# A three-stage float32 network on one core: norm roots on GpSimd, ordered weight subtractions, padded rows, another start

## The chip, the cores and the metric

One NeuronCore of one Trainium2 chip. TensorE (PE) multiplies, with a weight-load stream of its own (PEld); VectorE (DVE), ScalarE (ACT) and GpSimd (POOL) do the elementwise work; SyncE (SP) issues nearly all DMAs. The metric is the device time of one execution in microseconds; lower is better.

## The reference, cut to what matters

256 tokens of width 1024 pass a first block (gated linear attention and block attention, then a feed-forward that picks 16 of 16384 experts per head) and a second block of two layers. Everything is float32. Between the stages stands, eight times, the same norm:

```
def rmsnorm(x, w):
    y = x * rsqrt(mean(x * x, axis=-1) + 1e-6)
    return y * w
h = h + mixer(rmsnorm(h, mix_norm))
h = h + conv_glu_ffn(rmsnorm(h, ffn_norm))
h = h + sigmoid(rmsnorm(h, ple_norm) @ ple_gate) * (p @ ple_proj)
```

The order of the stages is: first mixer, norm, experts (peer), norm, mixer ab, norm, feed-forward 0, norm, gate stage (ple) 0, norm, mixer c, norm, feed-forward 1, norm, gate stage 1.

## The kernel before, in words

*Tiles.* The tokens lie in two tiles of 128 rows (tile 0 and tile 1), h[0] and h[1]. A stage's input is the normalised h, transposed and kept in two parts: xTh, rounded to PE's fast float32 format, and xTl, the rest (xT for both). The mixers' outputs go to mT in the same form and the feed-forward's hidden rows to hT.

*Weights.* wload (L102 to L114) brings a block of 128x1024 by DMA into a ring tile raw (512 KB), ACT copies it to hi in the fast format (L109), and DVE, or in the peer stage at times GpSimd, subtracts to get lo (L112). A product is made of three PE instructions: hi with the high part, lo with the high part, hi with the low part. xs (L169) has the tokens as the stationary operand and 512 weight columns streaming past (L199 to L201); ws (L245) has the weights stationary and 256 tokens streaming (L258 to L260); peer_v (L909) is like xs.

*The hand-over between stages.* The last products of a stage (hold) are made for tile 0 first and then for tile 1. When tile 0's sums are done they are added to h (add_epi, L269) and norm_tile (L314) starts: ACT squares two halves with a running sum (L320), rsqrt (L271) makes the reciprocal root on DVE from ten instructions on 128x1 (L278 to L288, a first guess by integer arithmetic and a polynomial), and DVE makes xn = h * r * weight in three cuts of 256, 256 and 512 columns (L326). turn then transposes xn on PE into PSUM (L338), ACT copies the high part to xTh (L292) and DVE subtracts the low part to xTl (L293); turn is deferred by some steps (D_N) or flushed. Then tile 1 follows. The next stage's first weight group is made for tile 0 before tile 1, so PE can start on tile 0 alone; feed-forwards start with ple_proj, which does not read xT.

*Order.* The program is written in emission order, and a scheduler of the tile framework puts each engine's instructions into one queue by its own estimate of when they are ready; earlier emitted work has the higher priority. Each queue then runs in order. A later subtraction of the next stage's weights (L112) can therefore stand inside a norm's root if the scheduler thinks it is ready there.

*The start.* load_x (L368) issues on SP, in this order: h[0], the identity, the norm weights broadcast to 128 partitions (norm_w, L309), two weight blocks, h[1], two more weight blocks; after them come the constants of the first block and the second weight group.

*Places in memory.* Tiles are laid out pool by pool in the order in which pools are opened; pads (wpad, tpad) exist in the weight ring's pool and in the pool of small tiles. After the peer stage a pool cc is opened for good (build, L1387 on) with kw (128x64) and sink (128x2x16), float32, and the pools of mixer ab, feed-forward 0, gate 0, mixer c, feed-forward 1 and gate 1 are opened on top of it; xT and the weight ring lie below it.

Of the kernel before, what the change touches and what calls it, by code (L numbers as in the profile page):

```python
# [9 lines left out]
F32 = mybir.dt.float32  # L10
F32R = mybir.dt.float32r
# [31 lines left out]
def f32(ap):  # L43
    return ap.bitcast(F32)


class Net:
    def __init__(self, ctx, tc, T):
        self.ctx, self.tc, self.nc, self.T = ctx, tc, tc.nc, T
        e = ctx.enter_context  # L50
        self.const = e(tc.tile_pool(name="const", bufs=1))
        self.res = e(tc.tile_pool(name="res", bufs=1))
        self.wp = e(tc.tile_pool(name="wp", bufs=1))
        self.tiny = e(tc.tile_pool(name="tiny", bufs=3))
# [6 lines left out]
        self.turn, self.wx = {}, None  # L61
        self.deferred = []
        self.lo_pattern = "V"
        self.u_pattern = "G"
        self.v_pattern = "VG"
# [33 lines left out]
        self.wx = None  # L99


    def wload(self, src, width=2048):  # L102
        nc = self.nc
        out = []
        for a in range(0, width, 1024):
            raw = self.ring("raw", F32)
            nc.sync.dma_start(raw, src[:, a:a + 1024])
            hi, lo = self.ring("hi", F32R), self.ring("lo", F32R)
            nc.scalar.activation(hi, raw, AF.Copy)  # L109
            eng = nc.vector if self.lo_pattern[self.lo_i % len(self.lo_pattern)] == "V" else nc.gpsimd  # L110
            self.lo_i += 1
            eng.tensor_tensor(lo, raw, f32(hi), op=ALU.subtract)  # L112
            out.append((hi, lo))
        return out  # L114

    def defer(self, ticks, f, norm=False):

# [48 lines left out]
            except StopIteration:  # L166
                gens.remove(x)

    def xs(self, xT, seq, epi, hold=0, norm=None, ready=()):  # L169
# [39 lines left out]
        for tt in range(2):  # L209
            if not tt and norm is not None:  # L210
                wb = self.norm_w(norm)
            if tt:
                self.flush_norm()
            for i in range(max(early, 0), len(order)):
                step(i, tt)
                yield
            if norm is not None:
                self.norm_tile(tt, wb)

    def preload(self, seq):  # L220
        return [x for src, width, _ in seq for x in self.wload(src, width)]

    def group(self, src, c):
        return [(src[q], 2048, [(c, 2 * q), (c, 2 * q + 1)]) for q in range(2)]
# [4 lines left out]

    def out_proj(self, xT, src, first, epi, hold, norm):  # L230

        g = self.xs(xT, self.cross(src, first) + self.cross(src, 1 - first), epi, hold, norm)
# [57 lines left out]

    def split(self, dh, dl, p):
        self.nc.scalar.activation(dh, p, AF.Copy)  # L292
        self.nc.vector.tensor_tensor(dl, p, f32(dh), op=ALU.subtract)  # L293

    def bcast(self, pool, src, name, w=D):
        t = pool.tile([P, w], F32, name=name)
# [14 lines left out]
        self.nc.sync.dma_start(wb, bass.AP(tensor=w.tensor, offset=w.offset, ap=[[0, P], [1, D]]))  # L311
        return wb

    def norm_tile(self, tt, wb):  # L314

        nc, h, pool, xT = self.nc, self.h, self.np_pool, self.xT
        ss = self.tiny.tile([P, 2], F32, tag="ss", name=self.nm("ss"))
        for c in range(2):
            junk = pool.tile([P, 512], BF, tag="junk", name=self.nm("junk"))
            nc.scalar.activation(junk, h[tt][:, c * 512:c * 512 + 512], AF.Square, scale=1.0 / 32, accum_out=ss[:, c:c + 1])  # L320
        r = self.rsqrt(1, ss[:, :1], add=ss[:, 1:])
        xn = []
        for k, n in NORM_CUTS:
            cs = slice(k * P, (k + n) * P)
            x = pool.tile([P, n * P], F32, tag=f"xn{n}", bufs=2, name=self.nm("xn"))
            nc.vector.scalar_tensor_tensor(x, h[tt][:, cs], r, wb[:, cs], op0=ALU.mult, op1=ALU.mult)  # L326
            xn.append((x, k, n))

        def turn():
            for x, k, n in xn:  # L330
                self.tsplit(x, xT, k, tt, n)
        self.defer(D_N[tt], turn, True)


    def tsplit(self, src, xT, k0, tt, n=4, pin=False):
        p = self.sm_ps()[:, :n * P]
        for j in range(n):
            x = self.nc.tensor.transpose(p[:, j * P:(j + 1) * P], src[:, j * P:(j + 1) * P], self.ident)  # L338
# [4 lines left out]
        self.split(xT[0][:, k0:k0 + n, t], xT[1][:, k0:k0 + n, t], p3)  # L343

    def headnorm(self, dst, src, H, w, pool):

# [15 lines left out]
    def consts(self):  # L362
        nc, T, c = self.nc, self.T, self.const
        self.ident = c.tile([P, P], F32, name="ident")
        nc.sync.dma_start(self.ident, T["c_ident"])


    def load_x(self, between=lambda: None):  # L368
        nc, T = self.nc, self.T
        self.h = h = [self.res.tile([P, D], F32, tag=f"h{t}", name=self.nm("h")) for t in range(2)]  # L370
        nc.sync.dma_start(h[0], T["x"][:P, :])
        self.consts()
        r = between()
        nc.sync.dma_start(h[1], T["x"][P:, :])
        return r

    def block1(self):
        T = self.T
        seq = self.group(T["w_in_xs"][0], 0)
        wb, ready = self.load_x(lambda: (self.norm_w(T["norm1_w"]), self.preload(seq[:1])))  # L380
        ready += self.preload(seq[1:])
        h = self.h
        with ExitStack() as st:
            self.psum(st, **PS1)
            pool = st.enter_context(self.tc.tile_pool(name="b1x", bufs=1, reuse_waits="tile"))
            mT = self.new_xT(pool, "mT")
            for tt in range(2):
                self.norm_tile(tt, wb)
            self.flush()
            xT = self.xT  # L390
# [695 lines left out]
    def hg_scores(self, qs, kk, b, lbt, reset, lmask, dmask, at, ax, t2, t4, pool):  # L1086

        nc = self.nc
# [295 lines left out]
    def build(self):  # L1384
# [3 lines left out]
        for f, *args in ((self.peer,), (self.mixer_ab, 0), (self.ffn, 0), (self.ple, 0, False),  # L1388
# [114 lines left out]
```

## Time and profile before

| | us |
|---|---|
| runs, median of 3 (lowest to highest) | 1665.56 (1662.08 to 1666.26) |
| profiled execution, its own time | 1669.8 |
| its span in the profile | 1667.9 |
| PE busy | 1622.6 (97%) |
| DVE busy | 1223.6 (73%) |
| ACT busy | 942.6 (57%) |
| POOL busy | 271.9 (16%) |

The span is the time from the first to the last instruction in the profile; the execution's own time includes what lies around it. PE counts as busy while a product is in the array, and products overlap: the distance of two starts tells the pace. The granted clock of 1.00 is TensorE's higher level.

### The profile page before, as it was taken

To read this page: it belongs to the slowest core of one execution; us is meant where nothing else is said; L and a number is where in the kernel's file an instruction comes from. 1 tells how busy PE (TensorE), PEld (TensorE's weight loads), DVE (VectorE), ACT (ScalarE), POOL (GpSimd) and SP (SyncE) were. 2 spreads that over 40 slices of the span, in tenths; PEclk is the share of its full clock that TensorE was granted. 3 is DMA by queue.
4 is the path that set the end of the run, shared out by engine and by line. 5 is a ranking of instruction groups with operands and counts; after the bars stand their busy time and mean duration, and the time that the engine had idled before them with its cause. 6 is when DMAs were issued, how large, how long until landed. Compare 5 with 4: busy or idle time off the path is not lost.

```text
span 1667.9 us, 27611 instructions
## 1 busy us (share of the span) xinstructions
PE 1622.6 (97%) x10592; PEld 1450.4 (87%) x10592; DVE 1223.6 (73%) x2300; ACT 942.6 (57%) x1435; POOL 271.9 (16%) x127
## 2 busy tenths in 40 slices
PE   6999999999999999999999999999999899999998
PEld 5877999999999988888888889769998677899986
DVE  7766597908999996655666568878894775688846
ACT  4555545456766665555555556556663555566633
POOL 1000499983333310000000000100000000000000
PEclk9999999999999999999999999999999998999999
DMA  7536456554444456557665554346665651465651
GB/s 262 174 126 193 161 167 198 167 166 140 140 149 130 145 171 196 194 191 239 203 192 195 192 183 149 127 138 191 192 196 185 219 168 58 128 189 185 185 189 62
DMA packets 83199, 285.07 MB, mean 171 GB/s; under 512 B 10555, under 2 KB 14588, under 8 KB 82940
## 3 DMA queue, kind: packets, MB, share of 16 engines
q1 hardware_dynamic: 83068, 283.31, 52.9%
q8 instruction: 83, 1.36, 0.3%
q14 instruction: 48, 0.39, 0.1%
HBM read 281.16 MB, written 2.12 MB: 170 GB/s over the span
## 4 chain that ended last, share of the span: by engine, by line
PE 79%; DVE 16%; ACT 2%; issue 1%; DMA 1%; SPq 0%; DVEq 0%; ACTq 0%
PE mm L909 21%; PE mm L258 11%; PE mm L259 11%; PE mm L260 11%; PE mm L199 6%; PE mm L201 6%; PE mm L200 6%; DVE h L869 5%; DVE lo L112 4%; DVE E L863 2%; DVE act L879 1%; PE sm L557 1%; PE sm L873 1%; PE sm L338 1%; PE sm L529 1%
## 5 line engine op out<-in xcount | busy, mean ns | idle before, releaser
L109 ACT ACTIVATE hi<-raw 128x1024 fp32r<-128x1024 f32 x513 | 541.7, 1058 | 343.4 <-PE mm L259 151.1
L112 DVE TENSOR_TENSOR lo<-raw,hi 128x1024 fp32r<-128x1024 f32 x417 | 512.0, 1230 | 196.1 <-ACT hi L109 193.8
L258 PE MATMUL mm<-xTh,hi 128*128 128x256 f32 x1992 | 560.4, 281 | 0.2
L259 PE MATMUL mm<-xTl,hi 128*128 128x256 f32 x1992 | 554.0, 278 | 0.0
L260 PE MATMUL mm<-xTh,lo 128*128 128x256 f32 x1992 | 553.8, 278 | 0.0
L258 PEld LDWEIGHTS mm<-xTh,hi 128*128 128x128 f32 x1992 | 375.4, 189 | 1.5 <-ACT xTh L292 0.7
L260 PEld LDWEIGHTS mm<-xTh,lo 128*128 128x128 f32 x1992 | 375.5, 189 | 0.2
L259 PEld LDWEIGHTS mm<-xTl,hi 128*128 128x128 f32 x1992 | 374.4, 188 | 0.5 <-DVE xTl L293 0.3
L112 POOL TENSOR_TENSOR lo<-raw,hi 128x1024 fp32r<-128x1024 f32 x96 | 249.1, 2610 | 241.2 <-ACT hi L109 230.8
L869 DVE TENSOR_TENSOR h<-E,gate 128x512 f32<-128x512 bf16 x64 | 116.0, 1814 | 1.8 <-PE sm L873 1.8
L199 PE MATMUL mm<-hi,xTh 128*128 128x512 f32 x256 | 105.8, 414 | 2.8 <-DVE ry L281 1.9
L200 PE MATMUL mm<-lo,xTh 128*128 128x512 f32 x256 | 102.6, 401 | 0.3 <-DVE lo L112 0.3
L201 PE MATMUL mm<-hi,xTl 128*128 128x512 f32 x256 | 102.4, 401 | 0.0
L868 ACT ACTIVATE h<-E 128x512 f32<-128x512 bf16 x64 | 72.4, 1134 | 43.3 <-DVE E L863 41.6
L1331 DVE SCALAR_TENSOR_TENSOR fc<-mm,cw,fc 128x255 f32<-128x255 f32 (+1 forms) x176 | 84.3, 479 | 3.1
L909 PE MATMUL mm<-hi,xTh 128*128 128x512 f32 x256 | 79.5, 391 | 1.5 <-DVE act L839 1.0
L863 DVE TENSOR_TENSOR E<-sel,iota 128x1024 bf16<-128x1024 bf16 x64 | 48.5, 796 | 43.7 <-POOL iota L857 38.1
L909 PE MATMUL mm<-hi,xTl 128*128 128x512 f32 x256 | 80.0, 393 | 0.0
L909 PE MATMUL mm<-hi,wl 128*128 128x512 f32 x256 | 79.8, 393 | 0.0
L909 PE MATMUL mm<-lo,xTh 128*128 128x512 f32 x256 | 79.5, 391 | 0.0
L909 PE MATMUL mm<-lo,wh 128*128 128x512 f32 x256 | 79.3, 391 | 0.0
L909 PE MATMUL mm<-hi,wh 128*128 128x512 f32 x256 | 79.1, 390 | 0.0
(294 smaller groups left out, 2306.8 us busy)
## 6 DMA issues: line engine op xcount, KB each, us to landing
raw<-in_peer_uT SPq DMA_DIRECT2D x128, 512.0 KB, 3.8
raw<-in_peer_v SPq DMA_DIRECT2D x128, 512.0 KB, 3.6
raw<-in_ffn_up_ws SPq DMA_DIRECT2D x88, 512.0 KB, 4.4
raw<-in_ffn_down_a SPq DMA_DIRECT2D x40, 512.0 KB, 4.5
raw<-in_w_in_xs SPq DMA_DIRECT2D x20, 512.0 KB, 4.7
raw<-in_ab_ws SPq DMA_DIRECT2D x16, 512.0 KB, 4.5
raw<-in_ple_gate_xs SPq DMA_DIRECT2D x16, 512.0 KB, 4.4
raw<-in_w_query_ws SPq DMA_DIRECT2D x12, 512.0 KB, 4.5
```

The source lines that it names most:

```text
L109: nc.scalar.activation(hi, raw, AF.Copy)
L112: eng.tensor_tensor(lo, raw, f32(hi), op=ALU.subtract)
L199: nc.tensor.matmul(p, xh[:, k, t], hi[:, w], start=n == 1 and kk == 0, stop=False)
L200: nc.tensor.matmul(p, xh[:, k, t], lo[:, w], start=False, stop=False)
L201: nc.tensor.matmul(p, xl[:, k, t], hi[:, w], start=False, stop=n == total[c] and kk == 1)
L258: nc.tensor.matmul(o, hi[:, w], xh[:, k, :], start=k == 0, stop=False)
L259: nc.tensor.matmul(o, hi[:, w], xl[:, k, :], start=False, stop=False)
L260: nc.tensor.matmul(o, lo[:, w], xh[:, k, :], start=False, stop=k == 7)
L863: v.tensor_tensor(E[q], x[:, :, None, :].to_broadcast([P, T1, P, T2]), iota[:, None].to_broadcast([P, T1, P, T2]), op=ALU.is_equal)
L869: v.tensor_tensor(B.rearrange("p t j -> p j t"), E[1][:, i], gate[:, None, t0:t0 + T2].to_broadcast([P, P, T2]), op=ALU.mult)
L909: nc.tensor.matmul(self.acc[tt][c], st_[:, t], mv[:, c * 512:c * 512 + 512], start=first and j == js[0] and i == 0, stop=j == last and i == 2)
L1331: v.scalar_tensor_tensor(c[:, o + sft:o + S], p[:, o:o + S - sft], cw[:, wi, j:j + 1], c[:, o + sft:o + S], op0=ALU.mult, op1=ALU.add)
```

## The change

Four things are changed.

1. Every norm but the first makes its root from one DVE instruction (sum plus epsilon) and one GpSimd instruction, a power with exponent -0.5 held in a 128x1 tile (expo, in the place of the pad tpad).
2. After tile 0's norm, all weight subtractions emitted later on DVE get an order dependency, without a semaphore, on tile 0's last xn (behind). At the end of an out_proj (ws=True), from tile 1's turn on, they stand behind tile 1's last low-part subtraction instead, but for one of them (free = 1).
3. The pool cc gets 128 bytes of padding per partition (cpad), and mixer ab reuses lbt (64 bytes) for ebl.
4. The start is written anew: h[0] comes in two halves, the identity and the norm weights (one row, 4 KB) on ACT's DMA queue; PE spreads the row over 128 partitions by a product with a row of ones into two PSUM banks; the four weight blocks' hi copies stand on ACT behind the squares of tile 0 (two) and tile 1 (two); GpSimd makes the first and third lo, DVE the second and fourth. The first norm keeps the old root.

```diff
-        self.tiny.tile([P, 56], F32, tag="tpad", bufs=1, name="tpad")
+        self.expo = self.tiny.tile([P, 56], F32, tag="tpad", bufs=1, name="expo")[:, :1]
+        self.nc.gpsimd.memset(self.expo, -0.5)
...
+    def wsplit(self, raw):
...
+        x = eng.tensor_tensor(lo, raw, f32(hi), op=ALU.subtract)
+        if self.behind is not None and eng is nc.vector:
+            if self.free:
+                self.free -= 1
+            else:
+                self.tc.add_manual_dep(x.ins, self.behind.ins.name, mybir.DependencyInfo(
+                    mybir.DependencyClass.NoSync, mybir.DependencyReason.DATA), reason="behind the norm")
...
-    def norm_tile(self, tt, wb):
+    def norm_tile(self, tt, wb, between=None, ws=False):
...
-        r = self.rsqrt(1, ss[:, :1], add=ss[:, 1:])
+        if between:
+            between()
+        if between:
+            r = self.rsqrt(1, ss[:, :1], add=ss[:, 1:])
+        else:
+            x, r = [self.tiny.tile([P, 1], F32, tag=f"r{c}1", name=self.nm("n" + c)) for c in "xy"]
+            nc.vector.scalar_tensor_tensor(x, ss[:, :1], EPS, ss[:, 1:], op0=ALU.add, op1=ALU.add)
+            nc.gpsimd.tensor_tensor(r, x, self.expo, op=ALU.pow)
...
+        if not tt and not between:
+            self.behind, self.free = last, 0
 
         def turn():
             for x, k, n in xn:
-                self.tsplit(x, xT, k, tt, n)
+                last = self.tsplit(x, xT, k, tt, n)
+            if tt and ws:
+                self.behind, self.free = last, 1
...
     def block1(self):
+        for c in range(2):
+            nc.sync.dma_start(h[0][:, c * 512:c * 512 + 512], T["x"][:P, c * 512:c * 512 + 512])
...
+                nc.scalar.dma_start(row, bass.AP(tensor=w.tensor, offset=w.offset, ap=[[0, 1], [1, D]]))
+                nc.gpsimd.memset(ones, 1.0)
+                self.consts()
+                raws = self.wstart(*seq[0][:2])
+                nc.sync.dma_start(h[1], T["x"][P:, :])
+                raws += self.wstart(*seq[1][:2])
+                wb = [self.mm_ps() for c in range(2)]
+                for c in range(2):
+                    nc.tensor.matmul(wb[c], ones, row[:, c * 512:c * 512 + 512], start=True, stop=True)
...
+            def first():
+                his(0, 1)
+                lo(nc.gpsimd, 0)
+
+            def second():
+                his(2, 3)
+                lo(nc.gpsimd, 2)
+            self.norm_tile(0, wb, first)
             self.flush()
+            keep(lo(nc.vector, 1))
+            self.norm_tile(1, wb, second)
+            lo(nc.vector, 3)
+            self.flush()
...
-        ebl = pool.tile([P, 4, 4], F32, name="ebl")
+        ebl = lbt
...
                 self.c_small = cc([P, 64], F32, name="kw"), cc([P, 2, 16], F32, name="sink")
+                cc([P, 32], F32, name="cpad")
```

## Rows read from the trace of the kernel before

**Rows 1.** The page: busy time of each engine, and the chain by engine.
```profile
PE 1622.6 (97%) x10592; PEld 1450.4 (87%) x10592; DVE 1223.6 (73%) x2300; ACT 942.6 (57%) x1435; POOL 271.9 (16%) x127
...
PE 79%; DVE 16%; ACT 2%; issue 1%; DMA 1%; SPq 0%; DVEq 0%; ACTq 0%
```

**Rows 2.** Windows, PE: stretch, its length, busy us (instructions), clock, DMA share, GB/s.
```profile
0.00:30.00 30.00, 16.88 (x66) 1.00 0.79 272
134.00:152.00 18.00, 14.43 (x59) 0.91 0.80 259
964.00:982.00 18.00, 15.83 (x69) 0.91 0.58 173
1105.00:1123.00 18.00, 16.27 (x70) 0.91 0.45 137
1299.00:1317.00 18.00, 16.37 (x76) 1.00 0.70 231
1326.00:1344.00 18.00, 13.51 (x57) 0.91 0.54 173
```

**Rows 3.** Timeline, DVE before feed-forward 0: start, duration, instruction [idle before, releaser].
```profile
1107.26 0.16 DVE L278 SCALAR_TENSOR_TENSOR rx<-ss 128x1 f32<-128x1 f32 x1 [0.85 <-ACT junk L320]
...
1108.37 1.23 DVE L112 TENSOR_TENSOR lo<-raw,hi 128x1024 fp32r<-128x1024 f32 x1
...
1112.05 1.53 DVE L326 SCALAR_TENSOR_TENSOR xn<-h,ry,nw 128x256 f32<-128x256 f32 x3
```

**Rows 4.** Timeline, PE at the same hand-over.
```profile
1106.22 0.40 PE L199 MATMUL mm<-hi,mTh 128*128 128x512 f32 x1
...
1110.42 0.40 PE L199 MATMUL mm<-hi,mTh 128*128 128x512 f32 x1
...
1112.67 0.81 PE L338 MATMUL sm<-ident,xn 128*128 128x128 f32 x4 [1.39 <-DVE xn L326]
```

**Rows 5.** Timeline, the start, all engines.
```profile
7.66 0.16 DVE L288 SCALAR_TENSOR_TENSOR ry<-rt,ry 128x1 f32<-128x1 f32 x1
...
9.03 0.48 DVE L326 SCALAR_TENSOR_TENSOR xn<-h,ry,nw 128x256 f32<-128x256 f32 x1 [1.22 <-DMA nw<-in_norm_w]
...
10.52 1.06 ACT L109 ACTIVATE hi<-raw 128x1024 fp32r<-128x1024 f32 x1 [4.50 <-DMA raw<-in_w_in_xs]
...
13.62 0.78 PE L199 MATMUL mm<-hi,xTh 128*128 128x512 f32 x1
...
29.44 0.62 PE L199 MATMUL mm<-hi,xTh 128*128 128x512 f32 x2
```

**Rows 6.** Timeline, PE: 512-column products with hT (42 apart) and xT (15 apart).
```profile
1244.77 0.40 PE L199 MATMUL mm<-hi,hTh 128*128 128x512 f32 x1
...
1254.57 0.40 PE L199 MATMUL mm<-hi,hTh 128*128 128x512 f32 x1
...
1308.99 0.39 PE L199 MATMUL mm<-hi,xTh 128*128 128x512 f32 x1
...
1312.42 0.39 PE L199 MATMUL mm<-hi,xTh 128*128 128x512 f32 x1
```

**Rows 7.** Windows, PE: 30 us inside each feed-forward's first half.
```profile
1150.00:1180.00 30.00, 30.00 (x267) 1.00 0.63 193
1500.00:1530.00 30.00, 30.00 (x257) 1.00 0.57 188
```

**Rows 8.** Lines, POOL: its shortest rows (busy us, mean ns, idle before).
```profile
L426 POOL TENSOR_TENSOR rt<-ropecs,qkw 128x64 f32<-128x64 f32 x4 | 1.4, 364 | 0.0
L1493 POOL MEMSET const-float32-0.0<- 128x1 f32 x1 | 0.1, 103 | 0.2 <-issue 0.2
```

**Rows 9.** Timeline, DVE and POOL in the peer stage.
```profile
382.56 2.40 POOL L112 TENSOR_TENSOR lo<-raw,hi 128x1024 fp32r<-128x1024 f32 x1 [3.33 <-ACT hi L109]
382.72 3.17 DVE L869 TENSOR_TENSOR h<-E,gate 128x512 f32<-128x512 bf16 x1
...
387.35 1.09 DVE L869 TENSOR_TENSOR h<-E,gate 128x512 f32<-128x512 bf16 x1
```

More of the change, by code (lines that the diff above doesn't have):

```diff
@@ L61, in __init__ @@
         self.turn, self.wx = {}, None
+        self.behind, self.free = None, 0
         self.deferred = []
@@ L99, in close_wx, with wstart @@
         self.wx = None
-    def wload(self, src, width=2048):
[L103 to L114, printed above, removed]
+    def wstart(self, src, width=2048):
+        raws = []
+        for a in range(0, width, 1024):
+            raws.append(self.ring("raw", F32))
+            self.nc.sync.dma_start(raws[-1], src[:, a:a + 1024])
+        return raws
+    def wsplit(self, raw):
+        nc = self.nc
+        hi, lo = self.ring("hi", F32R), self.ring("lo", F32R)
+        nc.scalar.activation(hi, raw, AF.Copy)
+        eng = nc.vector if self.lo_pattern[self.lo_i % len(self.lo_pattern)] == "V" else nc.gpsimd
+        self.lo_i += 1
+        x = eng.tensor_tensor(lo, raw, f32(hi), op=ALU.subtract)
[5 more added lines that the diff above has]
+                    mybir.DependencyClass.NoSync, mybir.DependencyReason.DATA), reason="behind the norm")
+        return hi, lo
+    def wload(self, src, width=2048):
+        return [self.wsplit(raw) for raw in self.wstart(src, width)]
     def defer(self, ticks, f, norm=False):
@@ L167, in merge, with xs @@
                 gens.remove(x)
-    def xs(self, xT, seq, epi, hold=0, norm=None, ready=()):
+    def xs(self, xT, seq, epi, hold=0, norm=None, ready=(), ws=False):
         nc = self.nc
@@ L217, in xs @@
             if norm is not None:
-                self.norm_tile(tt, wb)
-    def preload(self, seq):
-        return [x for src, width, _ in seq for x in self.wload(src, width)]
+                self.norm_tile(tt, wb, ws=ws)
     def group(self, src, c):
@@ L230, in out_proj @@
     def out_proj(self, xT, src, first, epi, hold, norm):
-        g = self.xs(xT, self.cross(src, first) + self.cross(src, 1 - first), epi, hold, norm)
+        g = self.xs(xT, self.cross(src, first) + self.cross(src, 1 - first), epi, hold, norm, ws=True)
         n = next(g)
@@ L319, in norm_tile @@
             junk = pool.tile([P, 512], BF, tag="junk", name=self.nm("junk"))
[L320 to L321 removed]
+            x = nc.scalar.activation(junk, h[tt][:, c * 512:c * 512 + 512], AF.Square, scale=1.0 / 32, accum_out=ss[:, c:c + 1])
+            if between:
+                self.tc.keep_in_program_order(x)
+        if between:
+            between()
+        if between:
+            r = self.rsqrt(1, ss[:, :1], add=ss[:, 1:])
[3 more added lines that the diff above has]
+            nc.gpsimd.tensor_tensor(r, x, self.expo, op=ALU.pow)
         xn = []
@@ L325, in norm_tile @@
             x = pool.tile([P, n * P], F32, tag=f"xn{n}", bufs=2, name=self.nm("xn"))
-            nc.vector.scalar_tensor_tensor(x, h[tt][:, cs], r, wb[:, cs], op0=ALU.mult, op1=ALU.mult)
+            w = wb[k // 4][:, (k % 4) * P:(k % 4 + n) * P] if isinstance(wb, list) else wb[:, cs]
+            last = nc.vector.scalar_tensor_tensor(x, h[tt][:, cs], r, w, op0=ALU.mult, op1=ALU.mult)
             xn.append((x, k, n))
+        if not tt and not between:
+            self.behind, self.free = last, 0
         def turn():
             for x, k, n in xn:
-                self.tsplit(x, xT, k, tt, n)
+                last = self.tsplit(x, xT, k, tt, n)
+            if tt and ws:
+                self.behind, self.free = last, 1
         self.defer(D_N[tt], turn, True)
@@ L364, in consts, with block1 @@
         self.ident = c.tile([P, P], F32, name="ident")
-        nc.sync.dma_start(self.ident, T["c_ident"])
-    def load_x(self, between=lambda: None):
+        nc.scalar.dma_start(self.ident, T["c_ident"])
+    def block1(self):
         nc, T = self.nc, self.T
+        seq = self.group(T["w_in_xs"][0], 0)
         self.h = h = [self.res.tile([P, D], F32, tag=f"h{t}", name=self.nm("h")) for t in range(2)]
[L371 to L382, printed above, removed]
+        xT = self.xT
+        for c in range(2):
+            nc.sync.dma_start(h[0][:, c * 512:c * 512 + 512], T["x"][:P, c * 512:c * 512 + 512])
         with ExitStack() as st:
@@ L386, in block1, with his, lo @@
             mT = self.new_xT(pool, "mT")
-            for tt in range(2):
-                self.norm_tile(tt, wb)
+            with self.tc.tile_pool(name="b1w", bufs=1, reuse_waits="tile") as pool:
+                row, ones = pool.tile([1, D], F32, name="nrow"), pool.tile([1, P], F32, name="ones")
+                w = T["norm1_w"]
+                nc.scalar.dma_start(row, bass.AP(tensor=w.tensor, offset=w.offset, ap=[[0, 1], [1, D]]))
[7 more added lines that the diff above has]
+                    nc.tensor.matmul(wb[c], ones, row[:, c * 512:c * 512 + 512], start=True, stop=True)
+            ready = [(self.ring("hi", F32R), self.ring("lo", F32R)) for _ in raws]
+            keep = self.tc.keep_in_program_order
+            def his(*js):
+                for j in js:
+                    keep(nc.scalar.activation(ready[j][0], raws[j], AF.Copy))
+            def lo(eng, j):
+                return eng.tensor_tensor(ready[j][1], raws[j], f32(ready[j][0]), op=ALU.subtract)
+            def first():
[5 more added lines that the diff above has]
+            self.norm_tile(0, wb, first)
             self.flush()
-            xT = self.xT
+            keep(lo(nc.vector, 1))
+            self.norm_tile(1, wb, second)
+            lo(nc.vector, 3)
+            self.flush()
             pool = st.enter_context(self.tc.tile_pool(name="b1", bufs=1, reuse_waits="tile"))
```

4 lines of the change are left out of this document (2 added, 2 removed).

## The prediction

> **What bounds the kernel now.** I read the page's busy shares and the chain that ended last first: TensorE (PE) is busy 97% of a span of 1667.9 us and holds 79% of the chain, VectorE (DVE) 16% [rows 1]. So there are two ways to gain: fill the few stretches in which PE waits, or make a PE instruction shorter. The change tries both, and each is read from its own view.
>
> The waits stand in a table of PE's busy time over the start and over the hand-overs where one stage's output is normalised for the next [rows 2]. There are seven hand-overs after the start; of 18 us each, PE is idle 3.57 (second norm of the first block), 2.17 (before the mixer ab), 1.73 (before the first feed-forward), 1.63 (before the first gate stage) and 4.49 us (before the mixer c); the second feed-forward and the second gate stage repeat the third and fourth row. Sum: 3.57+2.17+4.49+2x1.73+2x1.63 = 17.0 us. In five of the seven the granted clock averages 0.91: 18 x 0.09 = 1.6 us of full-speed time goes there to the lower of the two levels (1.2 instead of 2.4 GHz), some 8 us in all. The two gate stages, whose idle time is the shortest, keep the clock.
>
> What ends the wait is seen on DVE before the first feed-forward [rows 3]: the reciprocal root starts at 1107.26 and the first xn only at 1112.05, 4.8 us later. The root is ten dependent instructions of 0.15 us, about 0.19 apart (1.8 us alone); two weight subtractions of 1.23 us (one stands in the rows, the other starts at 1110.25) and two residual adds stand between them. PE's next work, the transposes of xn, comes at 1112.67 after 1.39 us of idle time that xn ended [rows 4]. The DVE's order, not its load, makes the wait.
>
> At the start [rows 5] the root is done at 7.82, but the first xn waits 1.22 us more, until 9.03, for the norm weights (512 KB written to 128 partitions, issued third on SP), ACT has idled 4.50 us when the first weight block lands at 10.52, and PE's first product is at 13.62. The second group's products start at 29.44.
>
> The length of a PE instruction shows in the distance of starts. Products of 512 columns whose stationary operand is hT lie (1254.57-1244.77)/42 = 233 ns apart; with xT (1312.42-1308.99)/15 = 229 ns [rows 6]; with mT before the feed-forward (1110.42-1106.22)/18 = 233 ns [rows 4]. Pools opened on the left after the peer stage stand behind kw and sink, 256+128 = 384 bytes; xT does not.
>
> **The change part by part.**
>
> *Padding.* 128 bytes more make that 512, so mT and hT of the later stages keep their distance to xT and to the weight ring modulo 512. If the 4.4 ns follow that distance, 528 products with hT (176 on each of three lines) and 192 with mT of ab and c gain: 720 x 4.4 ns = 3.2 us. Ends: 0 and 3.5. I take 3.2, since mT and hT, at the same base, show the same 233. Reusing lbt for ebl removes no instruction: 0.
>
> *Root as a power.* Nine of ten DVE instructions go, and one GpSimd (POOL) instruction on 128x1 comes. The trace has no power. From below, POOL's memset of 128x1 takes 0.10 us, the nearest two-input row (128x64) 0.36; from above I put one whole 128x1024 pass, 2.40 us [rows 8, 9]. I take 0.6 (128x64 and as much again for the function). POOL has nothing queued at the seven hand-overs, so its queue is free; behind the xn that now waits for POOL stand, on DVE, the residual adds of tile 1 and the weight subtractions, and PE waits for both.
>
> *Subtractions behind xn.* For tile 0 nothing but adds may stand before xn: 0.16+0.6+0.1 of hand-overs = 0.9 us in place of 4.8, so xn begins near 1108.2 instead of 1112.05 and ends (1.46 us for three) near 1109.7, before PE ends tile 1's products near 1111.2 (three after the one at 1110.42). The transposes then find their operand ready. What is late next: the two subtractions, 2.45 us, come after xn, at 1109.7 to 1112.1, and the next stage's second product needs the first. Then DVE has, before tile 1's operand is ready, four subtractions (4.9), six splits (2 x 1.3), two adds (1.2) and an xn (1.5): 10.2 us, against some 8 us of PE work (24 products of 0.229 and sixteen transposes after xn of tile 0). So waits don't vanish. I leave 0.85 us at six hand-overs and 1.5 at the second norm, where two waits stand in a row: 6.6 of 17.0 remain, 10.4 us gained. With idle stretches under the gate stages' 1.1 us, three of five low-clock stretches should go: 3 x 1.6 = 4.8. Sum 15.2. Ends: 5 (the subtractions only move the wait) and 22.
>
> *Start.* The weights come as one 4 KB row on ScalarE's (ACT) queue, spread by two PE products into PSUM; ident goes to that queue too, x in two halves. ACT's idle time hides both issues. xn then waits for the root alone (kept on DVE here): 7.8, or 7.3 with the first half's square begun early, against 9.03. With 0.5 MB less ahead of them the weight blocks land some 3 to 4 us sooner, first near 6.5, and PE's products start near 8.5 instead of 13.6. Two subtractions go to POOL, at 2.4 in place of 1.22 us; POOL's pass on the third block lets tile 0 end near 18 at the earliest, and tile 1 follows without subtractions inside its root: the second group starts near 25 instead of 29.4. I take 4.5 us; ends 2 and 6.5. SP issues fewer transfers ahead of the second group's blocks, so they aren't later.
>
> *Sum.* 15.2 + 4.5 + 3.2 = 22.9 us off the profiled execution (1669.8 us, span 1667.9), which stands 4.2 us above the median of the runs, 1665.56. The same off the median gives **1642.7 us**.
>
> **A rule weighed against the trace.** While POOL makes a 2.40 us subtraction, a DVE multiplication with two SBUF inputs takes 3.17 us instead of 1.09 [rows 9]; POOL and DVE hold each other up. The Trainium skill ("SBUF — State Buffer", Terms: shared port pair) states that the two arbitrate for one pair, held for a whole instruction, and that the loser blocks; by that rule, with which this trace agrees, the power may wait for a running subtraction. It gives the port rival below. With "behind" no subtraction can run beside tile 0's power; beside tile 1's it can.
>
> **The rivals.**
> - *Port* (0.12). Each tile 1 loses up to one subtraction of 1.22 us: 7 x 1.2 = 8.4 us, leaving 14.5 gained: 1651. For: rows 9. Against: tile 1's power need not meet a subtraction, and DVE is otherwise in use by the splits, whose one input is in PSUM.
> - *The wait only moves* (0.20). PE waits for the late subtractions instead of xn, and the low clock stays: 5 + 4.5 + 3.2 = 12.7 off: 1652.9. For: the DVE sum above is larger than PE's. Against: 2 x 1.6 us of DVE work are gone per hand-over.
> - *A slow power* (0.04), the slower side. Fourteen roots at no more than the 4.8 us of rows 3 make 67 us. With a power of T us the chains cost 14(T+0.3). From T = 5.0 they have eaten the 7.7 us gained elsewhere too; at T = 6 the kernel is 88-67-8 = 13 us slower: 1679. For: no row shows the function. Against: POOL's small rows are all under 0.6 us.
> - *The other pace* (0.18). Products of 256 columns with the same operands at the same addresses run at two paces: 267 starts in 30 us in the first feed-forward, 257 in the second [rows 7], 113 and 118 ns. What picks the pace the trace does not show; the moved instructions may flip it. 1056 products a feed-forward x 4.4 ns = 4.7 us: second becomes fast, 1638; first becomes slow, 1647.
> - *The padding does nothing* (0.04): the pace of hT products follows something else, 1646.
>
> **How the numbers follow.** The forecast itself has 0.42. A measurement of this kernel tells 0.3% (5 us) from no change. The slow power is slower (0.04), the worst of the moved wait and the port together could end within 5 us (0.05); the rest is faster (0.91). The range, 1630 to 1656, holds the forecast, the moved wait, port and both paces; below it lies the case that nearly all 25 us of waits and low clock go.
>
> **What would show it.** Right: xn begins about 1 us after the root's first instruction at tile 0 of all seven hand-overs; no weight subtraction stands between them; PE's idle time in the seven stretches falls from 17.0 us below 10; fewer stretches at 1.2 GHz; hT products 229 ns apart; PE's first product near 8.5 us. Wrong: a power over 2 us, PE waiting for L112's successor before the next stage's second product, hT products still at 233, or the start's gain given back before 60 us.

## The result: 1646.48 us against 1665.56, and the profile after

The changed kernel takes 1646.48 us, the median of 5 runs (1641.96 to 1647.94), against 1665.56: ratio 0.9878, 95% interval 0.9856 to 0.9899. That is 19.1 us off where 22.9 were forecast (1642.7, range 1630 to 1656). Six later runs of the same kernel had a median of 1651.65 beside a kernel before of 1667.19; over all 11 runs the changed kernel's median is 1647.9, over the 60 runs of the kernel before that stand beside the runs told of here, 1667.6. The profiled execution of the changed kernel (1641.96, span 1640.2) is the fastest of the eleven, the one of before (1669.8) slower than its median, so the two traces differ by 27.8 us, 8.7 more than the medians. A good part of what follows is about that difference.

The page, busy time and chain by engine, as [rows 1]:

```profile
PE 1607.5 (98%) x10596; PEld 1435.0 (87%) x10596; DVE 1206.6 (74%) x2172; ACT 943.2 (58%) x1435; POOL 290.2 (18%) x145
...
PE 80%; DVE 15%; ACT 2%; issue 1%; DMA 1%; POOL 1%; SPq 0%; DVEq 0%; ACTq 0%; POOLq 0%
```

TensorE is busy 15 us less than before: the same products, at a shorter distance or a higher clock.

Windows of PE over the seven hand-overs after the start, as [rows 2] (stretch, length, busy us and instructions, clock, DMA share, GB/s):

```profile
133.10:151.10 18.00, 16.55 (x80) 1.00 0.61 213
960.10:978.10 18.00, 16.26 (x73) 1.00 0.52 154
1100.20:1118.20 18.00, 17.38 (x94) 1.00 0.37 117
1290.30:1308.30 18.00, 17.03 (x79) 1.00 0.55 170
1317.60:1335.60 18.00, 16.47 (x76) 1.00 0.50 161
1414.00:1432.00 18.00, 17.34 (x95) 1.00 0.34 117
1602.70:1620.70 18.00, 17.03 (x79) 1.00 0.20 59
```

Idle time is 7 x 18 - 118.06 = 7.9 us, where [rows 2] gave 17.0. The granted clock is 1.00 (2.4 GHz) in all seven, where stretches of 3.41 us at the lower level (1.2 GHz, called half clock below) made it 0.91 in five.

The hand-over before the first feed-forward: DVE, POOL and PE, as [rows 3, 4]:

```profile
1103.08 0.16 DVE L339 SCALAR_TENSOR_TENSOR nx<-ss 128x1 f32<-128x1 f32 x1 [0.85 <-ACT junk L330]
1103.93 1.54 DVE L346 SCALAR_TENSOR_TENSOR xn<-h,ny,nw 128x256 f32<-128x256 f32 x3 [0.68 <-POOL ny L340]
...
1110.67 0.16 DVE L339 SCALAR_TENSOR_TENSOR nx<-ss 128x1 f32<-128x1 f32 x1
1110.74 1.22 DVE L117 TENSOR_TENSOR lo<-raw,hi 128x1024 fp32r<-128x1024 f32 x1
1112.40 0.48 DVE L346 SCALAR_TENSOR_TENSOR xn<-h,ny,nw 128x256 f32<-128x256 f32 x1 [0.44 <-POOL ny L340]
```
```profile
1103.32 0.57 POOL L340 TENSOR_TENSOR ny<-nx,expo 128x1 f32<-128x1 f32 x1 [32.32 <-DVE nx L339]
1110.90 1.47 POOL L340 TENSOR_TENSOR ny<-nx,expo 128x1 f32<-128x1 f32 x1 [7.01 <-DVE nx L339]
```
```profile
1104.56 0.81 PE L362 MATMUL sm<-ident,xn 128*128 128x128 f32 x4 [0.54 <-DVE xn L346]
```

Tile 0's xn starts 0.85 us after the root's first instruction (4.8 before), and its transposes fall between tile 1's products, after 0.54 us of idle time (1.39 before). The power takes 0.57 us there. At tile 1 it takes 1.47 while a weight subtraction runs on DVE from 1110.74, and xn starts 1.73 us after the root's first instruction (4.4 before).

The start, as [rows 5]: ACT, then DVE and POOL, then PE:

```profile
8.78 1.06 ACT L421 ACTIVATE hi<-raw 128x1024 fp32r<-128x1024 f32 x1 [3.31 <-DMA raw<-in_w_in_xs]
10.06 1.06 ACT L421 ACTIVATE hi<-raw 128x1024 fp32r<-128x1024 f32 x1 [0.23 <-DMA raw<-in_w_in_xs]
11.02 0.64 ACT L302 ACTIVATE xTh<-sm 128x256 fp32r<-128x256 f32 x2
```
```profile
6.52 0.55 DVE L297 SCALAR_TENSOR_TENSOR rt<-rt,rd 128x1 f32<-128x1 f32 x3
...
17.40 2.65 DVE L297 SCALAR_TENSOR_TENSOR rt<-rt,rd 128x1 f32<-128x1 f32 x3
```
```profile
16.99 2.37 POOL L424 TENSOR_TENSOR lo<-raw,hi 128x1024 fp32r<-128x1024 f32 x1 [4.72 <-ACT hi L421]
```
```profile
11.44 0.80 PE L212 MATMUL mm<-hi,xTh 128*128 128x512 f32 x1 [2.42 <-ACT xTh L302]
...
15.05 0.63 PE L214 MATMUL mm<-hi,xTl 128*128 128x512 f32 x1
15.47 0.63 PE L212 MATMUL mm<-hi,xTh 128*128 128x512 f32 x1
...
17.32 0.39 PE L213 MATMUL mm<-lo,xTh 128*128 128x512 f32 x1
17.55 0.39 PE L214 MATMUL mm<-hi,xTl 128*128 128x512 f32 x1
...
19.42 0.51 PE L213 MATMUL mm<-lo,xTh 128*128 128x512 f32 x1 [1.25 <-POOL lo L424]
...
29.18 0.62 PE L212 MATMUL mm<-hi,xTh 128*128 128x512 f32 x2
```

The first product comes 2.2 us earlier than in [rows 5], the second group's only 0.26. PE waits 1.25 us for a subtraction on POOL. While that subtraction runs (16.99 to 19.36), three steps of tile 1's root on DVE take 2.65 us, where tile 0's took 0.55; the first of them alone takes 1.98 and ends with the subtraction. The first products stand 0.42 us apart (15.05 to 15.47), later ones 0.23 (17.32 to 17.55). The trace's record of the granted clock begins only at 16.36 us, and in all fourteen traces the distance changes just where it begins, between 12.55 and 20.09 us. Where the record has half clock, such products stand 0.43 us apart (e1, from 82 us on). So the start runs at half clock until then; the 1.00 in the first line of [rows 2] stands for a stretch of which more than half (until 18.31) has no record.

### The profile page after: what moved, and what is told of

The parts are those of the page before. It is cut to its first block, busy times and chain, and to the rows that moved or that the text cites. A ratio compares the mean times of both kernels' runs of the same rounds, so it can differ in the third digit from the quotient of the medians.

```text
span 1640.2 us, 27505 instructions
## 1 busy us (share of the span) xinstructions
PE 1607.5 (98%) x10596; PEld 1435.0 (87%) x10596; DVE 1206.6 (74%) x2172; ACT 943.2 (58%) x1435; POOL 290.2 (18%) x145
## 4 chain that ended last, share of the span: by engine, by line
PE 80%; DVE 15%; ACT 2%; issue 1%; DMA 1%; POOL 1%; SPq 0%; DVEq 0%; ACTq 0%; POOLq 0%
PE mm L957 21%; PE mm L268 11%; PE mm L269 11%; PE mm L270 11%; PE mm L214 6%; PE mm L213 6%; PE mm L212 6%; DVE h L917 5%; DVE lo L117 3%; DVE E L911 2%; DVE act L927 1%; PE sm L921 1%; PE sm L605 1%; PE sm L362 1%; PE sm L577 1%
## 5 line engine op out<-in xcount | busy, mean ns | idle before, releaser
L117 DVE TENSOR_TENSOR lo<-raw,hi 128x1024 fp32r<-128x1024 f32 x413 | 506.0, 1230 | 172.9 <-ACT hi L114 169.8
L340 POOL TENSOR_TENSOR ny<-nx,expo 128x1 f32<-128x1 f32 x14 | 13.0, 925 | 928.2 <-DVE nx L339 928.2
```

The lines of the kernel that those rows point to most:

```text
L117: x = eng.tensor_tensor(lo, raw, f32(hi), op=ALU.subtract)
```

## The experiments

All but e10 and e11 start from the changed kernel. Times are medians; single runs of one kernel lie up to 19 us apart, so most of what follows is read from positions: all traces list the same 9144 products into mm banks, and the distance between two of them around a hand-over is compared with the same distance in the second trace of the changed kernel, e5. The table has the differences in us, worked out from starts; a plus is slower than e5. Where the padding is missing, gate 0 holds 1.0 us of it and gate 1 0.4. The columns ab and c are the mixers, f0 and f1 the feed-forwards:

```
                  norm2    ab    f0  gate0     c    f1  gate1
before            +3.81 +1.48 +3.01  +1.66 +3.85 +4.74  +0.87
e11 before again  +5.17 +0.14 +1.92  +1.66 +5.28 +4.72  +0.86
after, first     -0.02 +0.40 +0.03  -0.00 -0.01 -0.00  +0.01
e2 root on DVE    +1.44 +2.97 +0.59  +1.91 +4.17 +1.46  +1.73
e3 order undone   -1.12 -0.68 +0.96  -0.71 -0.73 +0.84  -0.77
e6 none free      -0.03 +0.00 +2.73  +0.01 -0.00 +1.72  -0.00
e8 power twice    +1.17 +1.25 +0.50  +1.08 +1.05 +0.03  +0.97
e9 order f0, f1   -1.11 -0.68 +0.03  -0.72 -0.73 +0.00  -0.78
e10 power alone   -1.00 -0.59 +0.98  +0.35 -0.74 +0.87  -0.38
```

**e1, padding undone.**

```diff
-        ebl = lbt
+        ebl = pool.tile([P, 4, 4], F32, name="ebl")
...
-                cc([P, 32], F32, name="cpad")
```

> The padding alone is undone: cpad goes and ebl has its own 64 bytes again; all else is as in the changed kernel. Theory A (the pace of a product follows the distance of its stationary operand to the other tiles modulo 512 bytes): the 528 products with hT and the 192 with mT of ab and c go back from 229 to 233.3 ns, 720 x 4.4 ns = 3.2 us, so 1649.7 against 1646.5. Rival B (the paces differ for another reason that came with the changed order of the instructions): the products stay at 229 and the time stays within 1 us of 1646.5.

1657.75 (1647.57 to 1660.6); ratio to before 0.9917, 0.9888 to 0.9947. The time says little, since the profiled execution also has 27 us at half clock and the first feed-forward at the slow pace of [rows 7]. The distance of the products decides. PE, two hT products 42 apart, in the changed kernel and in e1 (as [rows 6]):

```profile
1244.67 0.39 PE L213 MATMUL mm<-lo,hTh 128*128 128x512 f32 x1
...
1254.29 0.39 PE L213 MATMUL mm<-lo,hTh 128*128 128x512 f32 x1
```
```profile
1249.86 0.40 PE L213 MATMUL mm<-lo,hTh 128*128 128x512 f32 x1
...
1259.66 0.40 PE L213 MATMUL mm<-lo,hTh 128*128 128x512 f32 x1
```

9.62 / 42 = 229.0 ns and 9.80 / 42 = 233.3; mT of the two mixers goes back to 233.3 as well, xT stays at 229. So B falls, and the places in memory set the pace. That the distance modulo 512 bytes is the rule, as A has it, is not shown, since only these two layouts were run.

**e2, root on DVE; e3, order undone; e10, power alone on the kernel before.** The edits of e2 and e3 stand here; e10 puts the two lines that e2 removes into the kernel before, for the fourteen tiles of the norms after the first.

```diff
-            nc.vector.scalar_tensor_tensor(x, ss[:, :1], EPS, ss[:, 1:], op0=ALU.add, op1=ALU.add)
-            nc.gpsimd.tensor_tensor(r, x, self.expo, op=ALU.pow)
+        r = self.rsqrt(1, ss[:, :1], add=ss[:, 1:])
```
```diff
-        if self.behind is not None and eng is nc.vector:
+        if False:
```

> Every norm takes the ten-instruction root on VectorE again; the subtractions stay queued behind xn, padding and start stay. Theory A (order and power are worth about the same at a hand-over): tile 0's xn starts 1.9 us after the root's first instruction instead of 0.85, so each of seven hand-overs loses about 1 us at tile 0, and tile 1's root is cut by subtractions again: 7 x 1.0 to 7 x 1.5 = 7 to 10 us slower, 1653.5 to 1656.5, and some half-clock stretches come back. Rival B (the order does nearly all, as the operand is early by then): within 2 us of 1646.5. Rival C (the port: the power beside a subtraction costs 0.85 us at each tile 1, so the root on VectorE is no worse there): 1648 to 1650.

> The weight subtractions are no longer queued behind xn and xTl; power, padding and start stay. Theory A (order and power share the gain): with the root a single wait on POOL, a subtraction of 1.22 us slips in between x and xn, or beside the power at the shared port, at most hand-overs: xn starts 1.5 to 2.5 us after the root's first instruction, not 0.85; 7 x 1 us, 1651 to 1655. Rival B (the power does nearly all): within 2 us of 1646.5. Rival C (the order does nearly all): close to the kernel before without its padding gain, 1660 or more.

> The kernel before with one part of the change: at the fourteen norms after the first the root is a power on POOL; no order, no padding, old start. Theory A (the power makes nearly all of the hand-overs' gain): by positions the hand-overs gain 3.8+1.1 at the second norm, 2.1 at the mixer ab, 2.0 and 3.8 at the two feed-forwards, 1.3 and 0.8 at the two gate stages and 4.5 at the mixer c, 19 us together; the rest stays, so 1646 to 1652 with the run's paces, hT products at 233 ns. Rival B (power and order need each other): no more than 10 us at the hand-overs, 1656 or more.

e2: 1659.1, ratio 0.9934 (0.991 to 0.9958). e3: 1646.82, 0.9886 (0.9849 to 0.9922). e10: 1651.56, 0.9891 (0.9857 to 0.9924). Without the power, 14.3 us of the hand-overs come back (1.44+2.97+0.59+1.91+4.17+1.46+1.73), 5.1 of them by half-clock stretches (10.24 us). Without the order, 2.2 us are gained: 0.9 lost at each feed-forward, 0.7 to 1.1 gained at the five others. With the power alone the hand-overs cost what they do in e3, but for the padding. So the power does all of it. The parts don't add up: against the kernel before, both together gain 18.0 us at the hand-overs (its 19.4 in the table less 1.4 of padding), the power alone 19.9 (19.4 + 0.5) and the order alone 3.7 (18.0 less e2's 14.3). In the expectations, e2's theory A was too small, e3's A and C are wrong and B holds, and e10's A holds. In e3 no subtraction slips in between nx and tile 0's xn: 0.83 us at the second norm, 0.84 at the first feed-forward. The same is seen in e10, DVE at the first feed-forward:

```profile
1105.03 0.16 DVE L326 SCALAR_TENSOR_TENSOR nx<-ss 128x1 f32<-128x1 f32 x1 [0.85 <-ACT junk L321]
1105.88 1.54 DVE L332 SCALAR_TENSOR_TENSOR xn<-h,ny,nw 128x256 f32<-128x256 f32 x3 [0.68 <-POOL ny L327]
```

At tile 0 the scheduler puts nothing behind the one instruction; between the ten it did.

e2's DVE at tile 1 before the mixer c shows what ten leave: four subtractions inside the root (two stand in the rows), 5.8 us from 1334.22 to xn.

```profile
1334.22 0.15 DVE L288 SCALAR_TENSOR_TENSOR rx<-ss 128x1 f32<-128x1 f32 x1
1334.29 1.22 DVE L117 TENSOR_TENSOR lo<-raw,hi 128x1024 fp32r<-128x1024 f32 x1
1335.42 0.15 DVE L291 TENSOR_SCALAR ry<-rx 128x1 int32<-128x1 int32 x1
1335.49 1.22 DVE L117 TENSOR_TENSOR lo<-raw,hi 128x1024 fp32r<-128x1024 f32 x1
...
1340.05 1.54 DVE L341 SCALAR_TENSOR_TENSOR xn<-h,ry,nw 128x256 f32<-128x256 f32 x3
```

**e9, order at the feed-forwards only.**

```diff
-        if not tt and not between:
+        if not tt and ws:
...
-        g = self.xs(..., epi, hold, norm, ws=True)
+        g = self.xs(..., epi, hold, norm, ws=norm is not self.T["norm2_w"])
```

> The subtractions are queued behind xn and xTl only at the two hand-overs into a feed-forward; at the second norm, the mixers and the gate stages they run as the scheduler puts them; all else as in the changed kernel. Theory A (the order pays only where the next stage's first products need their subtractions at once behind a full set of weights; elsewhere it makes PE wait for a subtraction that could have gone earlier): against the second look at the changed kernel PE gains 1.1 us at the second norm, 0.7 at the mixer ab, 0.7 at each gate stage and 0.7 at the mixer c, and keeps both feed-forwards within 0.2 us: 4.0 us in all by positions of the products, 0.9969 of the changed kernel's time where the paces are alike. Rival B (the order's cost seen with it undone everywhere was an accident of that execution): positions within 0.5 us at each hand-over.

1642.2, ratio 0.9837 (0.9808 to 0.9866), beside 0.9878 and 0.9906 of the changed kernel's two sets. The hand-overs gain 1.11+0.68+0.72+0.73+0.78 = 4.0 us, each as expected. At the second norm, DVE behind tile 1's xn, in the changed kernel and in e9:

```profile
145.26 1.54 DVE L346 SCALAR_TENSOR_TENSOR xn<-h,ny,nw 128x256 f32<-128x256 f32 x3 [0.45 <-POOL ny L340]
146.72 2.36 DVE L117 TENSOR_TENSOR lo<-raw,hi 128x1024 fp32r<-128x1024 f32 x2
148.99 0.75 DVE L303 TENSOR_TENSOR xTl<-sm,xTh 128x256 fp32r<-128x256 f32 x2
```
```profile
144.37 1.54 DVE L346 SCALAR_TENSOR_TENSOR xn<-h,ny,nw 128x256 f32<-128x256 f32 x3 [0.45 <-POOL ny L340]
145.83 1.22 DVE L117 TENSOR_TENSOR lo<-raw,hi 128x1024 fp32r<-128x1024 f32 x1
147.29 1.46 DVE L303 TENSOR_TENSOR xTl<-sm,xTh 128x256 fp32r<-128x256 f32 x3 [0.24 <-ACT xTh L302]
```

The order lets none of the next stage's subtractions start ahead of tile 0's xn (in e9 one runs at 128.71), so two instead of one stand later between tile 1's xn and xTl; PE's two waits for a subtraction at this hand-over (0.31 and 0.63 us in the changed kernel) are gone in e9.

**e6, no subtraction free beside tile 1's power; e8, the power twice.**

```diff
-                self.behind, self.free = last, 1
+                self.behind, self.free = last, 0
```
```diff
-            nc.gpsimd.tensor_tensor(r, x, self.expo, op=ALU.pow)
+            nc.gpsimd.tensor_tensor(x, x, self.expo, op=ALU.pow)
+            nc.gpsimd.tensor_tensor(r, x, self.one, op=ALU.pow)
```

> At the two hand-overs into a feed-forward, the one subtraction that the change lets pass beside tile 1's power is queued behind tile 1's xTl too (the same at the second norm's tile 1, where it stood behind xn already); all else as in the changed kernel. Theory A (the port: a power beside a subtraction takes 1.4 us instead of 0.55): tile 1's power takes 0.57 at these two hand-overs and its xn starts 0.85 us after the root's first instruction instead of 1.73. But the second subtraction comes some 3 us later, so PE waits for it at the start of the feed-forward: net 0 to +1 us at each, 1646.5 to 1648.5. Rival B (the power is slow at tile 1 for another reason): it still takes 1.4 us. Rival C (the port's 0.85 us is all on the path and nothing waits for the subtraction): 1644.8.

> Each root is followed by a second power on POOL, to the exponent 1, so that each of the fourteen takes twice as long; the result is the same but for rounding. Theory A (the power is on the path that sets the end at most hand-overs): xn starts 0.6 us later at tile 0 and 0.6 to 1.4 us later at tile 1; PE's waits for xn grow by 0.4 to 1.2 us at each of seven hand-overs: 3 to 8 us, 1650 to 1655. Rival B (products of the other tile hide it): within 1.5 us of the changed kernel.

e6: 1650.43, ratio 0.9903 (0.9879 to 0.9926). POOL at the first feed-forward's tile 1, and PE behind it:

```profile
1114.81 0.55 POOL L340 TENSOR_TENSOR ny<-nx,expo 128x1 f32<-128x1 f32 x1 [7.00 <-DVE nx L339]
```
```profile
1120.82 0.39 PE L268 MATMUL mm<-xTh,hi 128*128 128x256 f32 x1 [0.75 <-ACT hi L114]
1121.74 0.39 PE L270 MATMUL mm<-xTh,lo 128*128 128x256 f32 x1 [0.42 <-DVE lo L117]
```

The same power on the same shape takes 0.55 us with no subtraction beside it and 1.47 with one, so it is the subtraction that holds it up, and B falls. The 0.9 us by which tile 1's xn comes sooner gain nothing: its transposes still follow PE's last products with pTh and pTl at once. But the subtraction that was moved is one the next stage needs, and the hand-overs get worse by 1.74 and 1.72 us of waits, more than A allowed. At the first a half-clock stretch (1122.56 to 1125.98) comes back and costs 1.6 more, of which the table's 2.73 holds 1.0. e8: 1653.11, ratio 0.9934 (0.991 to 0.9959); 6.0 us more at the hand-overs, of some 1.25 us of added power at each of seven (8.75 us). So two thirds of the added time are on the path, as theory A has it.

**e4, the old start; e7, the new start with all subtractions on DVE; e12, e9 with the start reordered.** e4 takes the start of the kernel before. e7 moves lo of blocks 0 and 2 from POOL to DVE, behind tile 0's splits, and hi of block 1 behind xTh. In e12, middle() runs between tile 0's second and third split; its core (blocks 2 and 3 are on DVE too):

```diff
             def first():
-                his(0, 1)
-                lo(nc.gpsimd, 0)
+                his(0)
+            def middle():
+                his(1)
+                keep(lo(nc.vector, 1))
...
-            self.norm_tile(0, wb, first)
-            self.flush()
-            keep(lo(nc.vector, 1))
+            self.norm_tile(0, wb, first, middle=middle)
+            keep(lo(nc.vector, 0))
+            self.flush()
```

> The start is the one of the kernel before (norm weights spread by the transfer, all four subtractions on VectorE, x in one piece, ident on SP's queue); the rest is the changed kernel. Theory A (from the traces: the first product 2.2 us earlier, but nothing of it left at the end of the first group's products): within 1 us of 1646.5. Rival B (the forecast's term: the start is worth 4.5 us, and was lost later for another reason): 1651. Rival C (the new start's subtractions on POOL cost more than the weights' spread gains): 1644 to 1645.5.

> The changed kernel with a start whose four subtractions are all on VectorE, behind the splits of tile 0, and with hi of the second block behind xTh of tile 0; the spread of the norm weights stays. Theory A (the new start gains nothing since POOL's two passes of 2.36 us and ScalarE's fixed order eat the 2.2 us by which the first product is earlier): PE's first product at about 10.3 instead of 11.4, no wait of 1.25 us for POOL's lo near 19, the second group starts near 27.2 instead of 29.2, and 1.5 to 2 us of it last to the second norm. Rival B (the half clock until 17 us and the arrival of the weights bound the start): the second group starts at 29.2 within 0.5 us.

> The kernel of e9 (order at the feed-forwards only) with a start in which VectorE makes the first subtraction between xn and the splits of tile 0 and the second between the splits, ScalarE makes the second hi after two of tile 0's three xTh, and the other two subtractions are on VectorE too; POOL makes none. Theory A (the new start gained nothing only because of where its subtractions stood): PE's first product at about 10.6, no wait over 0.5 us for a subtraction until tile 0 is done, the second group starts at 27.0 or earlier instead of 28.2 to 29.2, and at least 1 us of it is left at the second norm: 1641 against e9's 1642.2. Rival B (the arrival of the weights and the slow first products, 0.43 us apart instead of 0.23 until about 17 us, bound the start): the second group starts between 28 and 30 and nothing is left at the second norm.

e4: 1646.97, ratio 0.9874 (0.9841 to 0.9907). At product 300 (92.7 us in e5) the old start is 0.45 us behind e5 and 0.40 ahead of the changed kernel's first trace: the new start is worth nothing that can be told, as theory A has it. e7: 1650.63, 0.9887 (0.9866 to 0.9909), 0.88 behind e5 at product 300; the wait for POOL is gone and one of 2.54 us for DVE's first subtraction, kept behind the splits, takes its place. Its first weight block landed at 9.21, in e5 at 7.86, and its half clock lasts until 20.09, in e5 until 14.28, so e7 alone doesn't tell theory A from B. e12: 1641.77, 0.9819 (0.9789 to 0.9849). PE in e12:

```profile
9.53 0.79 PE L212 MATMUL mm<-hi,xTh 128*128 128x512 f32 x1
...
15.43 0.50 PE L213 MATMUL mm<-lo,xTh 128*128 128x512 f32 x1 [0.77 <-DVE ry L291]
...
20.28 0.89 PE L364 MATMUL sm<-ident,xn 128*128 128x128 f32 x4 [2.06 <-DVE xn L346]
...
27.25 0.39 PE L212 MATMUL mm<-hi,xTh 128*128 128x512 f32 x1
```

Its first block landed at 7.89, as in e9 (7.83), whose first product stands at 10.5 and second group at 28.2. One wait of 0.77 us (named ry, it ends with the subtraction of 1.23 us ahead of it) and the second group at 27.25 miss the letter of A by 0.3 us each, but 1.3 us against e9 are left at product 300, before the second norm, so A holds in the main: the order of ScalarE's and the subtractions' work at the start cost it. How much of the 1.3 us is the clock's is not separated, since the half clock ends at 12.55 in e12 and at 15.44 in e9; yet e5, where it ends at 14.28, is 0.1 us behind e9 and not ahead of it. Next late is tile 1's xn (2.06 us). Whether e12 beats e9 in time is open: the intervals overlap. e12's lies below both of the changed kernel's; e9's upper end, 0.9866, just overlaps the first of them, and what it gains rests on the positions.

**e5, the changed kernel again; e11, the kernel before again.** No edit.

> The changed kernel itself once more, unchanged, for a second profiled execution. Theory A (the half-clock stretches and the pace of the 256-column products belong to the execution, not to the program): against the first profiled execution of the same kernel (1642.0) the positions of the products differ by a few us, all of it in the mixer c (a half-clock stretch of 13.65 us, some 6.4 us) and in stages of 256-column products (1.1, 2.3 or 4.7 us), while each hand-over repeats within 0.2 us; times from 1641 to 1652. Rival B (the program fixes both): the positions repeat within 0.5 us throughout, the mixer ab at 118 ns and both feed-forwards at 113.

> The kernel before, unchanged, for a second profiled execution. Theory A (the half-clock stretches at its hand-overs follow its waits, while the long one in the mixer c and the pace of the 256-column products vary with the execution): stretches of 3.4 us again at the second norm, the mixer ab, the first feed-forward, the mixer c and the second feed-forward, hand-overs at the same positions within 0.3 us; the mixer's long stretch or the pace of one stage of 256-column products may differ (6.4 and 4.7 us). Rival B (the hand-overs' stretches are an accident of one execution too): two or more of the five are gone.

e5: 1651.65 (1646.19 to 1654.32), ratio 0.9906 (0.9887 to 0.9925). The hand-overs repeat within 0.03 us but for ab (0.40). The body of mixer c takes 5.6 us more than in the first trace, with 13.65 us at half clock; ten of the fourteen traces have such a stretch there. The stages of 256-column products have the first trace's paces, against the rest of theory A. But e4 and e7, which differ from the changed kernel in the first 30 us only, have others (e4: first feed-forward slow; e7: ab fast, second feed-forward slow), and over all traces the first feed-forward is fast in 10 of 14, the second in 9. In e2 the first changes from slow to fast within the stage. The kernel before shows both paces without any edit: 257 starts in the second feed-forward's window in [rows 7], 267 in e11 (last line below). So neither the stretch nor the pace is fixed by the program; what picks them stays open.

e11: 1666.48, ratio 0.9982 (0.9958 to 1.0006). Its windows at norm2, ab, the first feed-forward and c, where [rows 2] shows 0.91 at each, and one inside the second feed-forward, as [rows 7]:

```profile
134.00:152.00 18.00, 14.44 (x53) 0.81 0.75 256
965.00:983.00 18.00, 15.76 (x75) 1.00 0.59 173
1105.00:1123.00 18.00, 15.82 (x77) 1.00 0.41 130
...
1326.00:1344.00 18.00, 13.52 (x51) 0.81 0.54 170
...
1500.00:1530.00 30.00, 30.00 (x267) 1.00 0.66 195
```

Two of the five stretches are gone and two are twice as long. That is B by its letter, yet their sum is the same, 6.83+6.83+3.41 = 5 x 3.41 = 17.1 us. In the other twelve traces the hand-overs have a stretch only in e2 (two) and e6 (one), where PE waits longer than in the changed kernel. This speaks for the waits as their cause; which wait gets one varies.

## Why the prediction was right, and where it was not

**Padding, 3.2 us: right in the pace, 0.5 us high.** 233.3 to 228.9 ns for hT and mT; 720 x 4.4 ns. By positions e1 loses 1.10 and 1.13 us in the two hT stages and 0.18 and 0.26 with mT, 2.7 in all, where only about half of the mT products stand back to back. It isn't all that sets the pace: in e4, which has the padding, the first feed-forward's hT products took 233.3, in the stage whose 256-column products were slow as well (257 starts in 30 us, the slow pace of [rows 7]); the other 19 hT stages with padding took 228.9 to 229.0, and all eight without it 233.3.

**Hand-overs, 15.2 us: near in sum, wrong in part of the cause.** Measured 18.0 by positions (the first line of the table, 19.4, less 1.4 of padding; 18.3 by e11's line); by windows 9.1 of idle time (10.4 forecast) and five half-clock stretches of 3.41 us at half the cost, 8.5 (4.8 forecast, for three of five). The power at 0.6 us was 0.55 (the prediction's own words, 0.36 and as much again, make 0.72). The failed step is "Subtractions behind xn": the order was credited with keeping subtractions out from ahead of xn. e10 has none there without the order, e9 shows that the order costs 4.0 us at five hand-overs, and e3 that it earns 1.8 at the two feed-forwards. The rival that the wait only moves was thus real at a quarter of the gain's size, and its cause was the change's own order.

**Start, 4.5 us: wrong.** The first block landed at 8.78 (7.86 in e5), not near 6.5: the 0.5 MB that went from ahead of it are worth some 1.9 us at the 272 GB/s of [rows 2] (an estimate), which from 10.52 gives 8.6; no row shows the prediction's 3 to 4 us. ScalarE's fixed order put the second block's hi ahead of xTh, so the first product came at 11.44, not 8.5. The first products ran 0.42 us apart, at half clock, with which the prediction did not reckon. POOL's pass cost 1.25 us of PE; "Tile 0 ends near 18" had priced that pass, but not ACT's order. Tile 1's root, which was to be free of subtractions, took 5.0 us to xn, since the same pass held DVE up and a subtraction on DVE stood in between. By the second group the gain was given back, one of the prediction's own signs of being wrong. Of the 4.5, between -0.4 and +0.5 us is there at product 300; reordered (e12), 1.4 us against e5's start and 1.9 against e4's old one.

**Rivals.** *Port*: the power is held up at six of seven tiles 1, by 0.85 to 0.92 us and not 1.22. The Trainium skill ("SBUF — State Buffer", Terms: shared port pair) says that the loser of the pair blocks for the other's instruction; 0.55 against 1.47 us agrees. The time isn't to be had by moving the subtraction, since that one is needed first (e6). *Slow power*: no, 0.55. *Padding does nothing*: no, e1. *Other pace*: it happened in the profiled pair, the second feed-forward fast (-4.7) and ab slow (about +0.8), but the kernel before has the fast pace too (e11), so it is not the change's; what it does to the medians is not shown.

**Sum.** 18.0 + 2.7 + 0 = 20.7 us, where the medians of all runs say 1667.6 - 1647.9 = 19.7 and the first set 19.1; the rest is within what paces and stretches of single executions move. The forecast of 22.9 held 4.5 us too much at the start, 0.5 too much for the padding and 2.8 too little at the hand-overs. That it came within 4 us of the measured gain is in part luck, since these errors offset each other.

## What to carry to other kernels

A short chain of tiny instructions on a busy in-order engine costs what the scheduler puts between its links; cutting its length (19.9 us alone) beat pinning the order of what surrounds it (3.7 alone), and pinning is worth keeping only at the hand-overs where it is measured to pay. Before crediting one of two edits made together with a gain, run each alone. Where one execution can differ from the next by a half-clock stretch or a pace, compare positions of the same instruction in the traces before comparing times.

## What the runs showed of the hardware

- A power on GpSimd of 128x1 takes 0.55 us, 1.40 to 1.47 beside a DVE subtraction of 1.22 us. The other way round, a DVE step on 128x1 took 1.98 to 2.00 us beside a GpSimd subtraction of 2.37 to 2.39 in the eight traces that have one there, and 0.17 to 0.18 in the four with the old start.
- A half-clock stretch in mixer c comes in ten of fourteen traces; 13.65 us of it cost 5.6 us (e5) and 17.07 some 7.1 (e9). One of 10.24 us at 82 us comes in three (e1, e6, e10) and costs some 4.9.
- The first products go at the distance of half clock, 0.42 to 0.43 us, and at 0.23 from the moment on at which the record of the granted clock begins: 12.55 us in e12, 16.36 in the changed kernel's first trace, 20.09 in e7. Before that there is no record, and a granted clock of 1.00 printed for it says nothing.
- 256-column products at 113.3 or 117.8 ns and 512-column ones at 228.9 or 233.3 differ by the same 4.4 ns; in e4 both were slow in one stage. Whether they have one cause was not tried.
